# Weights of the first four column groups of each MLP split ahead, kept in DRAM, and loaded as hi and lo parts

## The chip, the cores and the metric

One core of one Trainium2 chip runs the kernel. Its engines are the matmul engine (PE), VectorE (DVE), ScalarE (ACT), GpSimd (POOL) and SyncE (SP), which issues the transfers. The metric is the time of one execution in microseconds on the device, as the median of several runs. All inputs and outputs lie in DRAM, in float32.

## What is computed

A decoder trunk of two layers over 1024 tokens of width 1024. Layer 0 mixes tokens by dilated attention in three head groups, layer 1 by gated linear attention (GLA); behind each mixer stands an MLP of width 4096 with a squared ReLU:

```python
def sq_relu_mlp(h, w_up, w_down):
    a = jax.nn.relu(h @ w_up)
    return (a * a) @ w_down

def reference(x, ...):
    for i in range(DEPTH):
        h = rmsnorm(x, norm_mix_w[i])
        if i % N_MIXERS == 0:
            x = x + dilated_attention(h, attn_w_in[j], attn_w_out[j])
        else:
            x = x + gla_mixer(h, gla_w_in[j], ...)
        h = rmsnorm(x, norm_mlp_w[i])
        x = x + sq_relu_mlp(h, mlp_w_up[i], mlp_w_down[i])
    return rmsnorm(x, final_norm_w)
```

The change concerns the first product of both MLPs, `h @ w_up`.

## The kernel before

**Arithmetic.** A float32 factor is cut in two: ACT rounds it to the short format that PE multiplies (`hi`), and DVE subtracts that from the factor (`lo`). A product is then three matmuls: hi with hi, hi with lo, lo with hi. The large products are moreover done in Strassen's way, as seven products P1 to P7 of quarter matrices in place of eight, so sums and differences of the factors' quarters have to be made first and sums of the products afterwards, on DVE.

**First product of an MLP** (class `Up`). The 4096 columns are done in 16 groups of 256. A group takes seven products of twelve matmuls, each 128x512, in the order P1, P2, P6, P5, P7, P4, P3 (numbered 0 to 6 in `product(p, s)`), into the banks X, Y, X, V, X, Z, V. Bank X is so used three times; between the uses ACT copies it out into a tile `e` (`copy`, line 634), and a product that wants X again waits for that copy. The sums go into `c11` (line 666), `rb` (lines 654 and 668) and `c12` (line 671); `squared` puts each through ReLU and a square on ACT (lines 638 and 639), and `sums` (lines 693 to 698) makes four more sums for the second product. `store` (line 686) writes all of it to DRAM, in `acts`.

**Weights of a group.** `load(p)` fetches the two raw tiles (line 546, 512 KB each), and `stage(p, s)`, in seven steps, makes the hi and lo parts: steps 0 and 1 cut the first column half (`wah`, `wal`), step 2 makes two differences (lines 594 and 595), step 3 cuts them (`wbh`, `wbl`), step 4 makes two more (lines 603 and 604), step 5 cuts those (`wgh`, `wgl`), and step 6 cuts one quarter (`wd`, which holds hi and lo). A cut is a rounding on ACT (line 566) and a subtraction on DVE (line 567).

**Order.** The program is written in the order in which it is to run: each engine executes its own instructions in the order of the code, and waits where one isn't ready. SP issues all transfers, in order too, with at most eight in flight. The stages are: value projections of the attention (class `Values`, 42 steps of 24 matmuls, `prep` of a step two steps ahead), attention heads, output projection (`out_proj`), first MLP (`Halves.finish`, then `Up.run`, then `Down`), then GLA and the same once more for the second MLP, with the final norm at the end of its `Down`. `Down` is the second product of an MLP, 56 steps of 24 matmuls; each step's two factors are loaded five steps ahead (`fetch`, `load`) and cut two steps ahead (`prep`, lines 219 and 222).

The rows of an MLP's input become ready only at the end of `out_proj`, in halves, so the sums of the activations (`s1`, `s2`, `s3`, `a22`, `s4`, lines 378 and 382) are made while the first products run. `Halves.finish` therefore interleaves the products of groups 0 to 3 by hand with these sums and with the staging of the groups' weights; the first groups' loads and first steps stand in `after(tb)`, in `out_proj`. `first_weights` and `first_stage` load and cut the first half of groups 2 and 3 separately. From group 3's P6 on, `Up.run` is a regular loop, with the staging of group p + 1 beside the products of group p.

**Tiles.** The pool `k4` (25 slots of 4 KB per partition) is a ring: raw tiles, weight parts, operand parts of `Down`, and more, each of which waits until the tile that had its slot is done with. `h8` has 12 slots of 8 KB, `t2` 8 of 2 KB; PSUM has 8 banks.

Of the kernel before, what the change touches and what calls it, by code (L numbers as in the profile page):

```python
# [9 lines left out]
F32 = mybir.dt.float32  # L10
F32R = mybir.dt.float32r
# [30 lines left out]
def hybrid_trunk(ctx, tc, x, norm_mix, norm_mlp, norm_fin, a_in, a_out, g_in, g_up, g_b, g_nw,  # L42
# [295 lines left out]
    class Halves:  # L338
# [85 lines left out]
        def after(self, tb):  # L424
            up = self.up
            if tb == 7:
                self.sum1(0)
            if tb % 2:
                self.norm(tb // 2)
            if tb == 1:  # L430
                up.load(0)
            elif tb == 2:
                up.load(1)
            elif tb == 3:
                up.stage(0, 0)
                up.stage(0, 1)
            elif tb == 4:
                up.stage(1, 0)
                up.stage(1, 1)
                up.first_weights(2)  # L440
                up.first_weights(3)
            elif tb == 5:
                up.stage(0, 2)

        def finish(self):
            up, a = self.up, self.a
            P1, P2, P6, P5, P7, P4, P3 = range(7)

            def split(name, src, lo):
                for c in range(2):  # L450
                    self.split(name, src, c, self.one, lo)

            up.product(0, P1)
            self.sum2(0)
            up.done(0, P1)
# [5 lines left out]
            up.first_stage(3)  # L461
            up.product(1, P2)
            up.product(2, P1)
# [20 lines left out]
            up.stage(0, 4)  # L484
            up.product(0, P5)
            split("s3", a[1, 0], self.two)
            up.done(0, P6)
            up.stage(0, 5)
            up.stage(0, 6)
            up.load(2)  # L490
# [5 lines left out]
            up.stage(1, 4)  # L496
            up.product(1, P5)
            up.stage(1, 5)
            up.product(0, P7)
            up.done(0, P7)  # L500
            up.product(0, P4)
            up.stage(1, 6)
            up.stage(2, 2)
            up.stage(2, 3)
            self.sum4()
            up.load(3)
# [4 lines left out]
            up.squared(0, P4)  # L511
            up.product(1, P4)
            up.add(1, P4)
            up.product(2, P6)
            up.stage(2, 4)
# [9 lines left out]
            up.sums(0)  # L525

    NP = FF // 256
    ORDER = ("a12", "a11", "s1", "s2", "s4", "s3", "a22")
# [2 lines left out]
    class Up:  # L531
# [3 lines left out]

        def __init__(self, i):
            self.w = m_up[i]
            self.count = NP
            self.h = {}
            self.raw, self.raw1, self.part, self.t, self.st = {}, {}, {}, {}, {}  # L540

        def load(self, p):
            if p < NP:
# [4 lines left out]
        def first_weights(self, p):  # L548

            if p % 2:  # L550
                r = [t2([P, 4, 128], F32, "raw1") for _ in range(2)]
            else:
                r = r6([P, 2, 4, 128], "raw1")
                r = [r[:, k] for k in range(2)]
            for k in range(2):
                sp.dma_start(r[k], cols(self.w, 256 * p, 128, 4 * k, 4))
            self.raw1[p] = r

        def first_stage(self, p):
            w = self.part.setdefault(p, {})  # L560
            w["a"] = self.two(F32R, "wah"), self.two(F32R, "wal")
            for k, r in enumerate(self.raw1.pop(p)):
                self.cut(*(t[:, k] for t in w["a"]), r)

        def cut(self, hi, lo, src):
            act.activation(hi, src, AF.Copy)  # L566
# [177 lines left out]
    xmid = drp.tile([S, D], F32, name="xmid")  # L744
    acts = [drp.tile([7, 2, P, 512], F32, name=f"acts{m}") for m in range(8)]
    vscr = drp.tile([S, NG, AW], F32, name="vscr")

    class Values:

# [237 lines left out]
    class Heads(Up):  # L987
# [3 lines left out]

        def __init__(self, h):
            self.h = h
            self.raw, self.raw1, self.part, self.t, self.st = {}, {}, {}, {}, {}
# [289 lines left out]
    for n in range(6, 8):  # L1284
# [7 lines left out]
        else:  # L1292
            for c in range(2):
                hs.cut("a22", c)
    vals.load(12)
    for n in range(8, vals.STEPS):
# [145 lines left out]
        st.finish()  # L1442


    class Down:

        def __init__(self, i, next_norm, spill):
            self.w = m_down[i].rearrange("(m j k p) c -> m k p j c", j=2, k=2, p=P)
            self.next_norm, self.spill = next_norm, spill
            self.sin, self.raw, self.cut = {}, {}, {}  # L1450
            self.br, self.tc, self.xs = [], [], [None] * 4
            self.acc = {}
            self.fin = {}
# [88 lines left out]
        def run(self):  # L1542
            ADDS = (None, ("B", 0, 0), ("A", 0, 0), ("B", 1, 1), ("A", 0, 1), ("B", 0, 1), ("A", 1, 0))
            for n in range(54):
                q, m = divmod(n, 8)
                if q and m < 4:
                    s, half, c = ADDS[q]
                    self.add(s, half, m, c)
                    if q == 6:
                        self.add(s, half, m, 1)  # L1550
                self.prep(n + 2)
                self.fetch(n + 5)
                self.load(n + 5)
# [377 lines left out]
```

## Time and profile before

| | us |
|---|---|
| median of 3 runs | 2676.93 |
| lowest and highest | 2676.9, 2678.23 |
| span of the profiled execution | 2672.2 |
| PE busy in it | 2625.7 |
| DVE, ACT, POOL busy | 1787.9, 1238.1, 92.2 |

The span runs from the first to the last instruction that the profile shows; 4.7 us of the median lie outside it. In lists of instructions each row gives the start and duration in us, the engine, the line, the operation and the tiles (output, arrow, inputs), and in brackets how long the engine stood idle before and for whom. Line numbers are those of the kernel before, unless the change is spoken of.

### The profile page before, as it was taken

The numbers are of one execution on the slowest core, as the hardware profiler recorded it, in microseconds if no ns is written. First come the engines' busy times: TensorE is split into PE (matmuls) and PEld (weight loads), VectorE is DVE, ScalarE is ACT, GpSimd is POOL, SyncE is SP. The second block draws the span as 40 slices with busy tenths as digits, with TensorE's granted clock in tenths as the row PEclk, the third lists the DMA queues.
The fourth block names the chain that finished last, engine by engine and source line by source line (L and its number), as shares of the span: only waits on it lengthen the run. The fifth ranks groups of instructions, "written<-read, shape, count | busy, mean of one in ns | idle before, by whom it ended". The sixth has DMA issues, their size and how long they took to land.

```text
span 2672.2 us, 33218 instructions
## 1 busy us (share of the span) xinstructions
PE 2625.7 (98%) x12248; PEld 2175.2 (81%) x12248; DVE 1787.9 (67%) x2944; ACT 1238.1 (46%) x2300; POOL 92.2 (3%) x72
## 2 busy tenths in 40 slices
PE   8999999999999999999999999999999999999998
PEld 6888888888888787888888887778888788888887
DVE  7645878888888677666565672562657766656567
ACT  6323455555555355555533343442425555553343
POOL 0000000000000000000000011321200000000000
PEclk9999999999999999999999999999999999999999
DMA  5443455565557534444856453011223444496543
GB/s 185 165 133 115 116 146 149 145 163 140 152 144 200 187 115 150 158 146 154 308 215 189 137 179 99 24 40 64 91 83 123 153 159 149 139 329 215 185 150 125
DMA packets 311411, 402.16 MB, mean 150 GB/s; under 512 B 18864, under 2 KB 183216, under 8 KB 311248
## 3 DMA queue, kind: packets, MB, share of 16 engines
q1 hardware_dynamic: 311248, 400.04, 47.6%
q8 instruction: 96, 1.57, 0.2%
q14 instruction: 67, 0.55, 0.1%
HBM read 267.13 MB, written 107.68 MB: 140 GB/s over the span
## 4 chain that ended last, share of the span: by engine, by line
PE 80%; DVE 11%; ACT 4%; issue 2%; DMA 2%; SPq 0%; DVEq 0%; ACTq 0%
PE pB L1518 13%; PE pX L629 12%; PE pA L1518 10%; PE pV L629 8%; PE pd L213 5%; PE pd L215 5%; PE pd L214 5%; PE pY L629 4%; PE pB L827 4%; PE pZ L629 4%; PE pA L827 3%; PE pO L960 1%; PE pS L919 1%; DVE c L1013 1%; DMA rows<-og 1%
## 5 line engine op out<-in xcount | busy, mean ns | idle before, releaser
L1518 PE MATMUL pB<-dh 128*128 128x512 f32 x512 | 199.4, 389 | 0.0
L1518 PE MATMUL pB<-dh,dl 128*128 128x512 f32 x512 | 199.2, 389 | 0.0
L1518 PE MATMUL pB<-dl,dh 128*128 128x512 f32 x512 | 199.2, 389 | 0.0
L222 DVE TENSOR_TENSOR dl<-sin,dh 128x1024 fp32r<-128x1024 f32 x112 | 136.6, 1219 | 43.0 <-ACT dh L219 42.5
L219 ACT ACTIVATE dh<-sin 128x1024 fp32r<-128x1024 f32 x112 | 117.8, 1052 | 89.7 <-PE pB L1518 33.5
L935 ACT ACTIVATE pt<-pt,orow 128x128 f32<-128x128 f32 (+1 forms) x192 | 85.0, 444 | 150.2 <-DVE orow L933 148.9
L219 ACT ACTIVATE dh<-kept 128x1024 fp32r<-128x1024 f32 x64 | 67.9, 1061 | 183.3 <-DVE kept L1483 138.0
L629 PE MATMUL pV<-s4h,wd 128*128 128x512 f32 x448 | 150.8, 398 | 0.4 <-ACT e L1050 0.4
L1518 PE MATMUL pA<-dh 128*128 128x512 f32 x384 | 149.4, 389 | 0.0
L1518 PE MATMUL pA<-dl,dh 128*128 128x512 f32 x384 | 149.4, 389 | 0.0
L1518 PE MATMUL pA<-dh,dl 128*128 128x512 f32 x384 | 149.4, 389 | 0.0
L567 DVE TENSOR_TENSOR wbl<-t,wbh 128x1024 fp32r<-128x1024 f32 x56 | 68.6, 1225 | 76.0 <-ACT wbh L566 76.0
L1518 PEld LDWEIGHTS pB<-dl,dh 128*128 128x128 f32 x512 | 96.1, 188 | 20.1
L1518 PEld LDWEIGHTS pB<-dh 128*128 128x128 f32 x512 | 96.1, 188 | 19.9
L1518 PEld LDWEIGHTS pB<-dh,dl 128*128 128x128 f32 x512 | 96.1, 188 | 19.8
L567 DVE TENSOR_TENSOR wal<-raw,wah 128x512 fp32r<-128x512 f32 x112 | 76.2, 686 | 47.8 <-ACT wah L566 47.8
L629 PE MATMUL pX<-s3h,wgh 128*128 128x512 f32 x224 | 93.2, 416 | 11.6 <-ACT e L634 11.6
L638 ACT ACTIVATE c<-c 128x512 f32<-128x512 f32 x64 | 40.4, 632 | 137.6 <-DVE c L666 83.1
L213 PE MATMUL pd<-whi,hTh 128*128 128x512 f32 x256 | 100.5, 393 | 0.0
L148 POOL TENSOR_TENSOR wlo<-raw,whi 128x1024 fp32r<-128x1024 f32 x16 | 40.0, 2500 | 1745.1 <-DMA raw<-in_gla_w_in_dram 1587.7
L215 PE MATMUL pd<-whi,hTl 128*128 128x512 f32 x256 | 99.7, 389 | 0.0
L214 PE MATMUL pd<-wlo,hTh 128*128 128x512 f32 x256 | 99.6, 389 | 0.0
(307 smaller groups left out, 7423.8 us busy)
## 6 DMA issues: line engine op xcount, KB each, us to landing
sin<-acts SPq DMA_DIRECT2D x112, 512.0 KB, 3.9
raw<-in_mlp_w_up_dram SPq DMA_DIRECT2D x64, 512.0 KB, 5.9
acts<-s SPq DMA_DIRECT2D x64, 512.0 KB, 3.4
raw<-in_mlp_w_down_dram SPq DMA_DIRECT2D x64, 512.0 KB, 4.6
raw<-in_attn_w_in_dram SPq DMA_DIRECT2D x96, 256.0 KB, 4.5
cw<-c SPq DMA_DIRECT2D x192, 128.0 KB, 2.3
acts<-c SPq DMA_DIRECT2D x64, 256.0 KB, 2.2
kept<-in_mlp_w_down_dram SPq DMA_DIRECT2D x32, 512.0 KB, 5.3
```

Source lines behind the costliest of these rows:

```text
L148: eng.tensor_tensor(lo, src, hi.bitcast(F32), op=OP.subtract)
L213: pe.matmul(ps, sh, mh, start=start, stop=False)
L214: pe.matmul(ps, sh, ml, start=False, stop=False)
L215: pe.matmul(ps, sl, mh, start=False, stop=stop)
L219: act.activation(hi, src, AF.Copy)
L222: dve.tensor_tensor(lo, src, hi.bitcast(F32), op=OP.subtract)
L567: self.remain(lambda: dve.tensor_tensor(lo, src, hi.bitcast(F32), op=OP.subtract))
L629: pe.matmul(st[b], u[:, k, :], v, start=first and k + n == 0, stop=k == 3 and n == 2, skip_group_check=True)
L638: act.activation(r, r, AF.Relu)
L827: pe.matmul(self.acc[s][t], a[:, c], b[:, k, :], start=fresh and m + k + v == 0, stop=m == 1 and k == 1 and v == 2, skip_group_check=True)
L935: act.activation(pt[:, i, :128 * n], pt[:, i, :128 * n], AF.Exp, scale=-1.0, bias=m, accum_out=self.row[:, r, HD:HD + 1])
L1518: pe.matmul(self.acc[s][t], a[:, k, c], b[:, k, :], start=fresh and m + k + v == 0, stop=m == 7 and k == 1 and v == 2, skip_group_check=True)
```

## The change

For groups 0 to 3 of both MLPs the staging is taken out of `out_proj`, `finish` and `run`. A new class `Ahead` does it in seven steps per group, 28 per MLP (line numbers 535 to 556 of the changed kernel): it loads the two raw tiles, makes the differences in place in them, cuts the same seven parts, and writes them to DRAM, seven tiles of 512 KB per group (`wpre`). A cut's subtraction on DVE and the stores behind it are put off to the next step. MLP 0's 28 steps stand in `Values`, one in each of its steps from 9 on, with the raw tiles in one `h8` slot; to free that slot the load of the rotary table `tab` moves from step 12 to step 38. MLP 1's stand in the `Down` of MLP 0, one in each of its steps 10 to 37, raw tiles in `k4`. `fetch(p, ...)` later loads the parts back: the `a` parts in `after(tb)`, the `b`, `g` and `d` parts in `finish`. `first_weights` and `first_stage` go. The load of group 4 moves from `run` into `finish`.

```diff
         def after(self, tb):
             if tb == 1:
-                up.load(0)
+                up.fetch(0, "a")
             elif tb == 2:
-                up.load(1)
-            elif tb == 3:
-                up.stage(0, 0)
-                up.stage(0, 1)
+                up.fetch(1, "a")
...
         def finish(self):
             up.product(0, P1)
             self.sum2(0)
             up.done(0, P1)
-            up.first_stage(2)
             up.product(0, P2)
-            up.stage(0, 3)
+            up.fetch(0, "b")
...
             up.squared(0, P2)
-            up.stage(1, 2)
-            up.stage(1, 3)
+            up.fetch(0, "g", "d")
...
             up.add(0, P4)
+            up.fetch(2, "g", "d")
             up.product(1, P7)
...
+            up.load(4)
             up.product(2, P5)
-            up.stage(2, 5)
-            up.stage(2, 6)
             up.product(0, P3)
+            up.fetch(3, "g", "d")
             up.product(1, P3)
...
+    class Ahead:
+            def load():
+                r["x"] = self.raw_tiles()
+                for k in range(2):
+                    sp.dma_start(r["x"][k], cols(self.w, 256 * p, 256, 4 * k, 4))
...
+            def cut(hi, lo, src, *stored):
+                act.activation(hi, src, AF.Copy)
+                def rest():
+                    dve.tensor_tensor(lo, src, hi.bitcast(F32), op=OP.subtract)
+                    if stored:
+                        put(*stored)
+                self.behind.append(rest)
...
+            def one():
+                pair("ah", "al")
+                cut(o["ah"][:, 0], o["al"][:, 0], block(0, 0))
+                cut(o["ah"][:, 1], o["al"][:, 1], block(1, 0), "ah", "al")
...
+            def three():
+                less(block(0, 0), block(0, 1), block(0, 0))
+                less(block(0, 1), block(1, 1), block(0, 1))
+                pair("bh", "bl")
+                cut(o["bh"][:, 1], o["bl"][:, 1], block(0, 0))
...
+            self.todo.extend((load, one, two, three, four, five, six))
+
+        def step(self):
+            late = list(self.behind)
+            self.behind.clear()
+            for fn in late:
+                fn()
+            if self.todo:
+                self.todo.popleft()()
...
+        def fetch(self, p, *names):
+            w = self.part.setdefault(p, {})
+            for n in names:
+                got = []
+                for part in ("d",) if n == "d" else (n + "h", n + "l"):
+                    t = self.two(F32R, "w" + part)
+                    sp.dma_start(t.bitcast(F32), self.ahead[p][PARTS.index(part)]
+                                 .rearrange("p (a b c) -> p a b c", a=2, b=4))
...
         def run(self, tail):
             self.product(2, 4)
-            self.stage(3, 2)
             self.product(2, 5)
             self.done(2, 4)
             self.done(1, 6)
-            self.stage(3, 3)
-            self.load(4)
             self.product(2, 6)
             self.done(2, 5)
-            self.stage(3, 4)
-            self.stage(3, 5)
             self.sums(1)
-            self.stage(3, 6)
...
     for n in range(8, vals.STEPS):
-        if n == 12:
+        if n >= 9:
+            ahead.step()
+        if n == vals.STEPS - 4:
             ctab = h8([P, 2, S], F32, "tab")
...
     class Down:
                 self.hook(n)
+                if self.ahead is not None and n >= 10:
+                    self.ahead.step()
                 self.product(n)
```

PE has the same instructions in the same order in both kernels. DVE's rows in MLP 0, from the sum c12 of group 1 (the first row) to that of group 2 (the last), read before, with group 3's staging (lines 567, 603 and 604) among them:

```order
L671 TENSOR_TENSOR c_9254<-pV,e_9031 128x512
L567 TENSOR_TENSOR wbl<-t,wbh 128x1024
L668 TENSOR_TENSOR rb<-pZ,e_9250 128x512
L603 TENSOR_TENSOR t<-raw 128x512
L604 TENSOR_TENSOR t<-raw,t 128x512
L567 TENSOR_TENSOR wgl<-t,wgh 128x1024
L693 TENSOR_TENSOR s_9289<-rb 128x512
L694 TENSOR_TENSOR s_9289<-s_9289,c_8925 128x512
L697 TENSOR_TENSOR s_9293<-c_8925,rb 128x512
L698 TENSOR_TENSOR s_9293<-c_9254,s_9289 128x512
L567 TENSOR_TENSOR wd<-raw,wd 128x512
L671 TENSOR_TENSOR c_9312<-pV,e_9162 128x512
```

In the changed kernel the same stretch of DVE, again from c12 of group 1 to c12 of group 2 (now line 733), reads:

```order
L733 TENSOR_TENSOR c_9409<-pV,e_9196 128x512
L730 TENSOR_TENSOR rb<-pZ,e_9405 128x512
L755 TENSOR_TENSOR s_9430<-rb 128x512
L756 TENSOR_TENSOR s_9430<-s_9430,c_9099 128x512
L759 TENSOR_TENSOR s_9434<-c_9099,rb 128x512
L760 TENSOR_TENSOR s_9434<-c_9409,s_9430 128x512
L733 TENSOR_TENSOR c_9450<-pV,e_9317 128x512
```

Five rows of staging are gone, and what is left are the sums of the products. SP's rows in `finish` of MLP 0 are, before, from the stores of c11 of groups 0 to 3 (line 686) to the first stores of group 0's other results:

```order
L686 DMA acts_82<-c_8923 128x512
L686 DMA acts_82<-c_8925 128x512
L686 DMA acts_83<-c_8964 128x512
L546 DMA raw<-in_mlp_w_up_dram 128x4x256 x2
L686 DMA acts_83<-c_9023 128x512
L546 DMA raw<-in_mlp_w_up_dram 128x4x256 x2
L686 DMA acts_82<-rb 128x512
L686 DMA acts_82<-c_9208 128x512
```

In the changed kernel (line 748 is the store, line 622 the loading back; `wp_1` is group 1), SP has from the stores of c11 of groups 1 and 2 on:

```order
L748 DMA acts_82<-c_9099 128x512
L748 DMA acts_83<-c_9137 128x512
L622 DMA wgh<-wp_1_gh 128x1024
L622 DMA wgl<-wp_1_gl 128x1024
L622 DMA wd<-wp_1_d 128x1024
L748 DMA acts_83<-c_9188 128x512
L622 DMA wbh<-wp_2_bh 128x1024
L622 DMA wbl<-wp_2_bl 128x1024
L622 DMA wgh<-wp_2_gh 128x1024
L622 DMA wgl<-wp_2_gl 128x1024
L622 DMA wd<-wp_2_d 128x1024
```

Group 2's parts moved in behind the last store of c11; behind them come group 3's, group 4's raw tiles and then the stores of group 0's other results. In `Down` of MLP 0, from the first step with a store on, SP of the changed kernel has (line 1527 loads a step's sin, line 1544 its weights):

```order
L543 DMA wp_0_ah<-ah 128x1024
L543 DMA wp_0_al<-al 128x1024
L1527 DMA sin<-acts_84 128x2x512
L1544 DMA kept<-in_mlp_w_down_dram 128x2x512
L543 DMA wp_0_d<-d 128x1024
L1527 DMA sin<-acts_85 128x2x512
L1544 DMA kept<-in_mlp_w_down_dram 128x2x512
L1527 DMA sin<-acts_86 128x2x512
L1544 DMA kept<-in_mlp_w_down_dram 128x2x512
L543 DMA wp_0_bh<-bh 128x1024
L543 DMA wp_0_bl<-bl 128x1024
```

The rows of line 543 are new there; each waits for its part's subtraction on DVE, and the loads of the steps behind it wait with it.

More of the change, by code (lines that the diff above doesn't have):

```diff
@@ L430, in after @@
             if tb == 1:
-                up.load(0)
+                up.fetch(0, "a")
             elif tb == 2:
-                up.load(1)
-            elif tb == 3:
-                up.stage(0, 0)
-                up.stage(0, 1)
+                up.fetch(1, "a")
             elif tb == 4:
[L438 to L443, printed above, removed]
+                up.fetch(2, "a")
+            elif tb == 6:
+                up.fetch(3, "a")
         def finish(self):
@@ L455, in finish @@
             up.done(0, P1)
-            up.first_stage(2)
             up.product(0, P2)
-            up.stage(0, 3)
+            up.fetch(0, "b")
             up.product(1, P1)
             self.turn(3)
-            up.first_stage(3)
             up.product(1, P2)
+            up.fetch(1, "b")
             up.product(2, P1)
@@ L487, in finish @@
             up.done(0, P6)
-            up.stage(0, 5)
-            up.stage(0, 6)
-            up.load(2)
+            up.fetch(1, "g", "d")
             up.product(1, P6)
@@ L495, in finish @@
             up.squared(3, P2)
-            up.stage(1, 4)
+            up.fetch(2, "b")
             up.product(1, P5)
-            up.stage(1, 5)
             up.product(0, P7)
@@ L511, in finish @@
             up.squared(0, P4)
+            up.fetch(3, "b")
             up.product(1, P4)
@@ L537, in __init__ @@
             self.w = m_up[i]
+            self.ahead = wpre[i]
             self.count = NP
             self.h = {}
-            self.raw, self.raw1, self.part, self.t, self.st = {}, {}, {}, {}, {}
+            self.raw, self.part, self.t, self.st = {}, {}, {}, {}
         def load(self, p):
@@ L546, in load @@
                     sp.dma_start(self.raw[p][k], cols(self.w, 256 * p, 256, 4 * k, 4))
[L548 to L559, printed above, removed]
-            w = self.part.setdefault(p, {})
-            w["a"] = self.two(F32R, "wah"), self.two(F32R, "wal")
-            for k, r in enumerate(self.raw1.pop(p)):
-                self.cut(*(t[:, k] for t in w["a"]), r)
+        def fetch(self, p, *names):
+            w = self.part.setdefault(p, {})
+            for n in names:
+                got = []
[3 more added lines that the diff above has]
+                                 .rearrange("p (a b c) -> p a b c", a=2, b=4))
+                    got.append(t)
+                w[n] = got[0] if n == "d" else tuple(got)
         def cut(self, hi, lo, src):
@@ L746, in hybrid_trunk @@
     vscr = drp.tile([S, NG, AW], F32, name="vscr")
+    wpre = [[[drp.tile([P, 1024], F32, name=f"wp{i}_{p}_{n}") for n in PARTS] for p in range(AHEAD)] for i in range(2)]
     class Values:
@@ L993, in __init__ @@
             self.h = h
-            self.raw, self.raw1, self.part, self.t, self.st = {}, {}, {}, {}, {}
+            self.raw, self.part, self.t, self.st = {}, {}, {}, {}
             self.count = HEADS * NG
@@ L1295, in hybrid_trunk, with raw_h8 @@
     vals.load(12)
+    def raw_h8():
+        t = h8([P, 2, 4, 256], F32, "praw")
+        return [t[:, k] for k in range(2)]
+    ahead = Ahead(0, raw_h8, wpre[0])
     for n in range(8, vals.STEPS):
-        if n == 12:
+        if n >= 9:
+            ahead.step()
+        if n == vals.STEPS - 4:
             ctab = h8([P, 2, S], F32, "tab")
@@ L1442, in out_proj, with raw_k4 @@
         st.finish()
+    def raw_k4():
+        return [k4([P, 4, 256], F32, "praw") for _ in range(2)]
     class Down:
@@ L1449, in __init__ @@
             self.next_norm, self.spill = next_norm, spill
+            self.ahead = Ahead(i + 1, raw_k4, wpre[i + 1]) if i == 0 else None
             self.sin, self.raw, self.cut = {}, {}, {}
```

38 lines of the change are left out of this document (32 added, 6 removed).

## The prediction

> **What bounds the kernel now.** The page comes first, for the share of each engine; then all waits of the matmul engine (PE); then windows of 50 us, to see in which stage PE is not full.
>
> ```profile
> span 2672.2 us, 33218 instructions
> PE 2625.7 (98%) x12248; PEld 2175.2 (81%) x12248; DVE 1787.9 (67%) x2944; ACT 1238.1 (46%) x2300; POOL 92.2 (3%) x72
> ...
> PE pT L366 <- DVE xn L256: 12.0, 7, 10.6
> PE pX L629 <- ACT e L634: 11.6, 2, 5.8
> PE pX L629 <- DVE wbl L567: 1.1, 2, 0.5
> ...
> 1000.00:1050.00 50.00, 49.47 (x217) 40.13 (x216) 39.76 (x56) 31.06 (x40) 0.00 (x0) 1.00 0.37 123
> 1050.00:1100.00 50.00, 44.23 (x186) 36.32 (x186) 34.91 (x52) 23.84 (x36) 0.00 (x0) 0.93 0.56 189
> 1100.00:1150.00 50.00, 50.00 (x222) 41.42 (x221) 30.87 (x45) 25.56 (x37) 0.00 (x0) 1.00 0.39 131
> 2100.00:2150.00 50.00, 43.67 (x183) 34.73 (x183) 35.03 (x51) 24.75 (x34) 0.00 (x0) 0.93 0.57 194
> ```
>
> PE is busy for 98% of the span, so work taken off DVE or ACT is worth only what PE waits for it. The first wait (12.0 us, 10.6 in one piece) is the start of the program, which the change leaves alone. The next two are what it touches: two waits of 5.8 us, one per MLP, for line 634 (ACT's copy that empties bank pX), and two of 0.5 for a low part of line 567. In a window row, behind the stretch and its length, stand the busy times of PE, weight loads, DVE, ACT and GpSimd, then the granted clock, the DMA share and GB/s. Outside the two stretches PE fills its window at clock 1.00; inside it has 44 of 50 us, at 0.93. So the change can win back one place in each MLP, and elsewhere it can only cost.
>
> The place, from the timelines of PE, ACT and DVE:
>
> ```profile
> 1040.60 0.68 DVE L671 TENSOR_TENSOR c<-pV,e 128x512 f32<-128x512 f32 x1
> 1042.52 1.04 ACT L566 ACTIVATE wbh<-t 128x1024 fp32r<-128x1024 f32 x1
> 1043.59 1.23 DVE L567 TENSOR_TENSOR wbl<-t,wbh 128x1024 fp32r<-128x1024 f32 x1 [2.31 <-ACT wbh L566]
> 1043.61 0.50 PE L629 MATMUL pX<-s2h,wbh 128*128 128x512 f32 x1
> 1047.28 0.39 PE L629 MATMUL pV<-s1h,wbh 128*128 128x512 f32 x1
> 1048.58 1.23 DVE L567 TENSOR_TENSOR wgl<-t,wgh 128x1024 fp32r<-128x1024 f32 x1 [1.97 <-ACT wgh L566]
> 1049.72 0.69 DVE L693 TENSOR_TENSOR s<-rb 128x512 f32<-128x512 f32 x1
> 1052.26 0.69 DVE L567 TENSOR_TENSOR wd<-raw,wd 128x512 fp32r<-128x512 f32 x1
> 1052.86 0.68 DVE L671 TENSOR_TENSOR c<-pV,e 128x512 f32<-128x512 f32 x1
> 1053.58 0.63 ACT L638 ACTIVATE c<-c 128x512 f32<-128x512 f32 x1 [4.51 <-DVE c L671]
> 1055.30 0.58 ACT L634 ACTIVATE e<-pX 128x512 f32<-128x512 f32 x1
> 1055.92 0.80 PE L629 MATMUL pX<-s3h,wgh 128*128 128x512 f32 x1 [5.77 <-ACT e L634]
> ...
> 1055.92 5.19 PE pX L629 x12
> 1061.12 2.72 PE pZ L629 x12
> ```
>
> I write 3P7 for product P7 of group 3. 3P7 needs pX, which the copy e (1055.30) empties of 3P6. That copy has had its data since 3P6 ended at about 1047; it stands on ACT behind the square of group 2's c12 (1053.58), and that square waits 4.51 us for the DVE add at 1052.86. DVE could have done this add as soon as group 2's P3 was in its bank, at 1043.6, where 3P6 begins. It stands behind the staging of group 3's weights: between 1043.59 and 1052.86 each cut on DVE waits for a rounding on ACT, and the roundings stand on ACT behind squares that wait for DVE. The two engines go in turns, both with idle time, and PE pays: 5.77 us of waiting, then twelve matmuls that take 5.19 us, where the twelve after them take 2.72.
>
> **What goes.** Loss of the stretch = first matmul of 3P4 (pZ) less first of 3P6, less three products of 2.72. MLP 0: 1061.12 - 1043.61 - 8.16 = **9.35 us** (0.95 in 3P6, where wbl is late; 5.92 before 3P7; 2.47 in the slow matmuls). MLP 1, from the same two matmuls:
>
> ```profile
> 2106.72 0.50 PE L629 MATMUL pX<-s2h,wbh 128*128 128x512 f32 x1
> 2119.03 0.80 PE L629 MATMUL pX<-s3h,wgh 128*128 128x512 f32 x1 [5.80 <-ACT e L634]
> 2123.34 0.40 PE L629 MATMUL pZ<-a22h,wgh 128*128 128x512 f32 x1
> ```
>
> 2123.34 - 2106.72 - 8.16 = **8.46 us**. Together 17.8. PE's instructions and their order are the same in both kernels, so this is all that can be won.
>
> Is all of it won? The staging of groups 0 to 3 leaves DVE: per group two cuts of 1.23 and seven operations of 0.69 us, 7.3 us, 29 us per MLP, most of it in the interleaved part ahead of this place. What is left in front of the copy, from 1040.6 on, at DVE's pitch of 0.6 us (1052.26 to 1052.86): group 2's P4 sum, ready when PE ends that product, at 1043.61 - 2.72 = 1040.9; its two passes on ACT of 1.04 each (as wbh, equally wide), to about 1044; four sums on DVE, not waited for; the c12 add at 1043.7 to 1044.3; its two passes on ACT, to 1045.7; then the copy, which now waits for 3P6 itself: 1046.33 to 1046.95 at unbroken pace. 3P7 is due at 1043.61 + 2 x 2.72 = 1049.05. That leaves 2.1 us, so I book both losses as gone. With the gap goes the slow clock: the twelve matmuls before it had no gap and the window row shows 1.00.
>
> By the Trainium skill (TensorE: Matmul & The Clock Gate, on the clock's activity window), an idle window of about 3.4 us halves the clock until PE has been busy as long again. The trace agrees: after 5.77 us twelve matmuls took 5.19 instead of 2.72. By that rule a gap shortened to 2 us would cost only itself; by a rule in proportion it would cost 2.9. With the gap gone both give the sum below; they differ for a late fetch, the second rival.
>
> **What is added, by place.** Per group there are 11 DVE and 7 ACT operations on 512 columns, 2 loads and 7 stores of 512 KB; so per MLP 44 x 0.69 = 30 us of DVE, 28 x 0.6 = 17 us of ACT, 4.2 MB read and 14.7 MB written, over 28 steps of 5.44 us = 152 us. Later come 28 loads, 14.7 MB.
>
> ```profile
> 72.00:232.00 160.00, 160.00 (x707) 132.50 (x706) 81.56 (x86) 49.99 (x67) 0.00 (x0) 1.00 0.41 136
> 1295.00:1349.00 54.00, 54.00 (x240) 44.72 (x239) 36.96 (x36) 29.05 (x30) 0.00 (x0) 1.00 0.96 351
> 1349.00:1509.00 160.00, 160.00 (x707) 132.48 (x707) 93.02 (x86) 57.23 (x56) 0.00 (x0) 1.00 0.55 181
> ...
> 250.00:300.00 50.00, 50.00 (x233) 41.68 (x232) 36.78 (x66) 17.35 (x37) 0.00 (x0) 1.00 0.45 124
> ...
> L827 PE MATMUL pB<-dl,s4h 128*128 128x512 f32 x48 | 18.8, 391 | 0.5 <-DVE dl L812 0.5
> L222 DVE TENSOR_TENSOR dl<-sin,dh 128x1024 fp32r<-128x1024 f32 x112 | 136.6, 1219 | 43.0 <-ACT dh L219 42.5
> ```
>
> *Value projections* (MLP 0's part): DVE 82 + 30 = 112 of 160 us, ACT 50 + 17 = 67, transfers 136 + 18.9 MB / 152 us = 260 GB/s. All three fit beside a PE that is full and that DVE feeds with steps of its own to spare. The one wait of PE there is 0.5 us, for a dl (its group's row above). I book 0; bounds -0.5 (that wait goes, since the table load moves from step 12 to 38) and +2 (it comes once for each group).
>
> *Down product of MLP 0* (MLP 1's part, steps 10 to 37): DVE 93 + 30 = 123 of 160, ACT 57 + 17 = 74, transfers 181 + 124 = 305 GB/s. The stage's first 54 us carry 351 GB/s at share 0.96 with PE full, so the rate has been sustained here without harm. What gets thinner is the lead of the split tiles: with raw tiles and pairs of the new work in the same ring of 25 slots, a step's splits wait for the slots of the product three steps before it where now they wait for one four or five before. That leaves two steps, 10.9 us, for splits of two roundings (1.04 each) and two cuts (1219 ns in the row above), some 5 us with a sum. I book +1, bounds 0 and +20 (four groups of 5 us).
>
> *Loading back.* SP issues in order, so a fetch stands behind the stores of c11 ahead of it, at about the times these have now.
>
> ```profile
> 942.15 0.38 SPq L354 DMA_DIRECT2D xmid<-xs  x1
> 979.21 0.39 PE L629 MATMUL pX<-a11h,wah 128*128 128x512 f32 x1
> 998.77 7.52 SPq L686 DMA_DIRECT2D acts<-c  x3
> 1013.64 0.39 PE L629 MATMUL pX<-s3h,wgh 128*128 128x512 f32 x1
> 1014.19 0.34 SPq L686 DMA_DIRECT2D acts<-c  x1
> ...
> sin<-acts SPq DMA_DIRECT2D x112, 512.0 KB, 3.9
> raw<-in_mlp_w_up_dram SPq DMA_DIRECT2D x64, 512.0 KB, 5.9
> ...
> sin<-acts SPq DMA_DIRECT2D x12, 512.0 KB, 8.8
> ```
>
> The a parts are asked for from 942 on and needed at 979. Group 0's g and d follow the store at 998.8, land at about 1006, and 0P7 needs them at 1013.64. Tightest is group 2's b: behind the last c11 store, at 1014.6, landing at 1020.5 (5.9, the price of an equal raw load); 2P6 comes four products after 0P7, at 1013.64 + 10.88 = 1024.5. That leaves 4 us, and still 1 at the 8.8 us that the most crowded loads took (the last row, of window 1295 to 1349). Group 3's parts are needed 19 us or more later. Booked at 0; bounds 0 and +6 for both MLPs.
>
> **Sum.** -17.8 + 0 + 1 + 0 = -16.8. The profiled execution's span of 2672.2 and 4.7 around it are 2676.9, the median itself: 2676.9 - 16.8 = **2660 us**.
>
> **Rivals.**
> 1. *Half is given back in Down.* Four times the rounding of a group's first half stands on ACT before its raw tile has landed, and the steps' own roundings behind it. It is asked for one step earlier, late in that step's work, and lands after 6 to 9 us, so ACT may stand for 4 to 8 us where the slack is 5 or 6. For: the thin ring. Against: sin, of the same size, lands in 3.9 over the whole kernel. At 2 to 4 us per group: 2659 + 8 to 2659 + 16, **2667 to 2675**.
> 2. *A late fetch takes the place of the stall*: group 2's b or g lands 3 us late in each MLP, 6 us in all, **2666**; were the slow clock to come with it, 2 us more each time (2.47 and less above), 2670. Against: the 4 us above.
> 3. *The stall stays*: the copy e is late for a reason that is not staging, say a square that waits for a store's buffer, or group 4's staging, which stays and whose raw load now comes behind fetches. Then the two gaps shrink by a few us at best: **2672 to 2677**. Against: all DVE work between 1043.59 and 1052.86 but the four sums is staging.
> 4. *Slower: Down becomes bound by its transfers.* The 28 steps then need 181 x 0.1523 = 27.6 + 18.9 = 46.5 MB in 152 us. Below 305 GB/s PE waits; at 273 GB/s the whole gain is gone (46.5 / 0.273 = 170 us); below 266 the kernel is over 0.2% slower. Window 250 to 300, with small packets, has 124 GB/s at share 0.45, that is 275 when full; stores mixed among loads could go as low. At 262 GB/s: 177.5 us, +25, **2685**. Against: 181 / 0.55 = 329 GB/s in this very stage.
>
> **Chances.** Forecast 0.62 (its own range 2656 to 2664), given back 0.16, late fetch 0.04, stall stays 0.08, slower 0.10. A measurement of this kernel can tell about 0.2%, 5.4 us, from no change, so faster means below 2671.5: 0.62 + 0.04 + 0.11 of the case given back = 0.77; same 0.05 + 0.08 = 0.13; slower 0.10. The range, 2656 to 2672, takes in the forecast, the late fetch and most of what is given back, some 0.78.
>
> **What would show it.** Right: no wait of PE on pX for e in either MLP, PE at 50.0 of 50 and clock 1.00 in 1050 to 1100, DVE's add for group 2's c12 within a us of 1043.6, and Down's 56 steps still at 5.44 us. Wrong: a PE wait for dl or dh in Down, or steps longer than 5.44 us at DMA share near 1 (rivals 1 and 4); a PE wait whose releaser is a DMA into wbh or wgh (rival 2); the old wait for e (rival 3). What would undo the forecast outright is PE waiting in the value projections, where I book nothing.

## The result, and the profile after

| | before | changed |
|---|---|---|
| median, us (4 runs each) | 2677.14 | 2657.98 |
| lowest and highest | 2676.9, 2678.23 | 2657.38, 2659.44 |
| span of the profiled execution | 2672.2 | 2655.9 |

The ratio is 0.9925, with a 95% interval of 0.9911 to 0.9939: faster by 0.75%, 19.2 us of the medians and 16.3 us of the two spans. The forecast was 2660.

From the page of the changed kernel come the span and the engines' shares; the next rows are the longest waits of PE over the whole span (in total, times, longest), and the last two are the windows of the two places, which the earlier start of MLP 1 has moved.

```profile
span 2655.9 us, 33487 instructions
PE 2622.3 (99%) x12248; PEld 2174.9 (82%) x12248; DVE 1789.6 (67%) x2960; ACT 1238.6 (47%) x2316; POOL 91.3 (3%) x72
...
PE pT L366 <- DVE xn L256: 11.7, 7, 10.3
PE pd L214 <- DVE wlo L148: 2.3, 3, 1.8
PE pk L1906 <- DVE kdT L1901: 2.0, 1, 2.0
...
1050.00:1100.00 50.00, 50.00 (x221) 41.20 (x220) 30.98 (x45) 26.13 (x38) 0.00 (x0) 1.00 0.49 163
2080.00:2130.00 50.00, 50.00 (x221) 41.23 (x220) 32.18 (x48) 24.90 (x34) 0.00 (x0) 1.00 0.64 225
```

DVE and ACT have as much to do as before; what is gone are the waits on pX, and PE fills both places at clock 1.00. The timelines of DVE, ACT and PE in MLP 0 show how (line 733 is the sum c12, first of group 1, then of group 2; line 696 copies pX):

```profile
1039.40 0.68 DVE L733 TENSOR_TENSOR c<-pV,e 128x512 f32<-128x512 f32 x1
1043.42 0.69 DVE L760 TENSOR_TENSOR s<-c,s 128x512 f32<-128x512 f32 x1
1044.02 0.68 DVE L733 TENSOR_TENSOR c<-pV,e 128x512 f32<-128x512 f32 x1
1044.74 0.63 ACT L700 ACTIVATE c<-c 128x512 f32<-128x512 f32 x1 [0.98 <-DVE c L733]
1046.46 0.58 ACT L696 ACTIVATE e<-pX 128x512 f32<-128x512 f32 x1
...
1043.40 0.39 PE L691 MATMUL pX<-s2h,wbh 128*128 128x512 f32 x1
1051.56 0.39 PE L691 MATMUL pZ<-a22h,wgh 128*128 128x512 f32 x1
...
2099.03 0.39 PE L691 MATMUL pX<-s2h,wbh 128*128 128x512 f32 x1
2107.19 0.39 PE L691 MATMUL pZ<-a22h,wgh 128*128 128x512 f32 x1
```

Group 2's c12 comes 4.6 us behind group 1's, where it came 12.3 behind, and the copy of pX is over at 1047.04, before 3P7 wants the bank. From 3P6 to 3P4 PE takes 1051.56 - 1043.40 = 8.16 us, in MLP 1 2107.19 - 2099.03 = 8.16: three products without a gap.

The stages that took over the work, in the windows that the prediction used:

```profile
72.00:232.00 160.00, 160.00 (x708) 132.56 (x707) 107.85 (x130) 64.98 (x95) 0.00 (x0) 1.00 0.75 258
1349.00:1509.00 160.00, 160.00 (x708) 132.51 (x707) 125.03 (x134) 72.05 (x83) 0.00 (x0) 1.00 0.84 292
```

PE is full in both, with DVE up by 26 and 32 us and the transfers at 258 and 292 GB/s. The work was not saved; it went to where it costs nothing.

### The profile page after: what moved, and what is told of

Same layout as the page of the kernel before. It is cut to its first block, busy times and chain, and to the rows that moved or that the text cites. A ratio compares the mean times of both kernels' runs of the same rounds, so it can differ in the third digit from the quotient of the medians.

```text
span 2655.9 us, 33487 instructions
## 1 busy us (share of the span) xinstructions
PE 2622.3 (99%) x12248; PEld 2174.9 (82%) x12248; DVE 1789.6 (67%) x2960; ACT 1238.6 (47%) x2316; POOL 91.3 (3%) x72
## 4 chain that ended last, share of the span: by engine, by line
PE 87%; DVE 7%; ACT 2%; issue 2%; DMA 2%; SPq 0%; DVEq 0%; ACTq 0%
PE pX L691 15%; PE pB L1586 13%; PE pA L1586 10%; PE pV L691 10%; PE pd L213 5%; PE pd L215 5%; PE pd L214 5%; PE pY L691 5%; PE pZ L691 5%; PE pB L884 4%; PE pA L884 3%; PE pS L976 2%; PE pO L1017 1%; DVE c L1070 1%; DMA rows<-og 1%
## 5 line engine op out<-in xcount | busy, mean ns | idle before, releaser
L696 ACT ACTIVATE e<-pX 128x512 f32<-128x512 f32 x96 | 56.5, 589 | 104.5 <-PE pX L691 104.5
L629 DVE TENSOR_TENSOR wbl<-t,wbh 128x1024 fp32r<-128x1024 f32 x48 | 58.8, 1225 | 66.9 <-ACT wbh L628 66.9
L691 PEld LDWEIGHTS pV<-s4h,wd 128*128 128x128 f32 x448 | 84.2, 188 | 18.7 <-ACT e L1107 1.3
```

Of the source, the lines that this page charges most:

```text
L629: self.remain(lambda: dve.tensor_tensor(lo, src, hi.bitcast(F32), op=OP.subtract))
L691: pe.matmul(st[b], u[:, k, :], v, start=first and k + n == 0, stop=k == 3 and n == 2, skip_group_check=True)
L696: act.activation(e, self.st[p]["X"], AF.Copy)
```

## Experiments

Both kernels' PE work is the same, so where a run loses or gains can be read from the start of each matmul, counted from the first, in two traces. That matters, since the attention heads alone shift by up to 3 us from one trace to the next. Each run was timed on one chip beside the kernel before. The question of the first three: is it group 3's staging that blocks (theory A), or the amount of work (theory B)?

**Only group 3 ahead.** The kernels here hold both ways of getting a group's weights, and a list says which groups go ahead:

```diff
-    AHEAD = 4
+    AHEAD = ((3,), (3,))
```

> Only group 3 of each MLP is split ahead and loaded back; groups 0 to 2 are staged in place as before. Theory A (the two waits on pX come from group 3's staging alone, which stands on DVE and ACT between the sums c12 of groups 1 and 2): nearly the whole gain, 15 to 18 us of the span, PE waiting under 1 us per MLP. Theory B (what counts is how much DVE work leaves the stretch, whichever group's): a quarter of the gain, 4 to 6 us.

Measured: 2657.7 us against 2676.66, ratio 0.9928 (0.9913 to 0.9943); PE has no wait in either MLP. This is the whole gain, with 415.8 MB moved in place of 458.8 (402.2 before): a quarter of the added traffic. Theory A holds against B.

**Groups 0 to 2 ahead, group 3 in place.**

```diff
-    AHEAD = 4
+    AHEAD = ((0, 1, 2), (0, 1, 2))
```

> Groups 0 to 2 are split ahead, group 3 is staged in place as before. Theory A: the turns of DVE and ACT over group 3's three cuts remain; by hand the copy of pX comes at about 1053.5 to 1054.1 where it came at 1055.3 to 1055.9, so the wait is still 4 to 5 us per MLP with the slow clock behind it, and 2 to 5 us are gained in all, most of it in 3P6. Theory B: three quarters of the gain, 12 to 14 us.

Measured: 2673.23 us against 2676.66, ratio 0.999 (0.998 to 0.9999), some 3 us, which is A's size; in the traces 2.2 us of it lie in the two MLPs. The waits on pX did not shrink to 4 or 5 us as expected, though. The rows (PE's waits, DVE, ACT; line 788 is c12 there, line 751 the copy, line 684 a cut's low part):

```profile
PE pX L746 <- ACT e L751: 11.4, 2, 5.8
...
1034.99 0.69 DVE L788 TENSOR_TENSOR c<-pV,e 128x512 f32<-128x512 f32 x1 [6.20 <-PE pV L746]
1044.67 1.23 DVE L684 TENSOR_TENSOR wbl<-t,wbh 128x1024 fp32r<-128x1024 f32 x1 [2.31 <-ACT wbh L683]
1049.66 1.23 DVE L684 TENSOR_TENSOR wgl<-t,wgh 128x1024 fp32r<-128x1024 f32 x1 [1.97 <-ACT wgh L683]
1054.65 0.63 ACT L755 ACTIVATE c<-c 128x512 f32<-128x512 f32 x1 [4.51 <-DVE c L788]
1056.37 0.58 ACT L751 ACTIVATE e<-pX 128x512 f32<-128x512 f32 x1
```

Three quarters of the staging are gone, and DVE has nothing to do for 6.2 us before it meets group 0's c12. Then it runs through the same turns with ACT (2.31, 1.97, 4.51 us of waiting, the very numbers of before) and the copy is as late as ever. Work taken out ahead of a place where the engine waits for PE anyway only makes that wait longer.

**The same, with group 3's staging written into that idle time.** Nothing is taken away against the run before:

```diff
             up.product(1, P3)
+            for k in range(2, 7):
+                up.stage(3, k)
             up.add(0, P3)
...
         def run(self, tail):
             self.product(2, 4)
-            self.stage(3, 2)
             self.product(2, 5)
```

(and so for steps 3 to 6 in `run`.)

> Groups 0 to 2 split ahead as in the run before; group 3 is staged in place, but its steps 2 to 6 are written ahead of the sum c12 of group 0, where the run before has DVE idle for 6.2 us (1028.8 to 1035.0). No work is taken away against that run. Theory A (what costs is that group 3's staging stands between the sums of groups 1 and 2): both waits on pX go, 15 to 18 us gained against the kernel before, as with all four groups ahead. Theory B (it is the amount of DVE and ACT work of the whole stretch): no gain over that run, 0 to 4 us against the kernel before.

Measured: 2663.28 us against 2677.45, ratio 0.9948 (0.9934 to 0.9963), 14.2 us, a little under A's 15 to 18. The waits on pX are down to 0.5 us in all; 1.7 and 1.5 us are left at the next place, where PE waits for rb of group 3. So, with groups 0 to 2 ahead, it is the place of this work that counts, not its amount in the whole stretch.

**Can order alone do it, with nothing ahead?** The kernel before, with `run` written in another order:

```diff
             self.done(2, 4)
-            self.done(1, 6)
             self.stage(3, 3)
+            self.done(1, 6)
             self.load(4)
             self.product(2, 6)
-            self.done(2, 5)
             self.stage(3, 4)
             self.stage(3, 5)
-            self.sums(1)
-            self.stage(3, 6)
+            self.done(2, 5)
+            self.product(3, 2)
+            self.add(2, 6)
+            self.done(3, 2)
+            self.squared(2, 6)
+            self.stage(3, 6)
+            self.sums(1)
...
```

> The kernel before, nothing split ahead; only the written order of the run of groups 2 and 3 is changed: group 3's roundings stand on ACT ahead of the squares of groups 1 and 2, the add of c12 of group 2 and the copy of pX ahead of that square, and the four sums of group 1 behind. Theory A in its strict form (it is the place in the queues, not the amount of work): the copy of pX ends by about 1048, so 14 to 18 us are gained with no byte moved. Theory B (DVE and ACT are too full there): under 6 us.

Measured: 2681.93 us, ratio 1.0015 (1.0005 to 1.0024): no gain, rather a loss. The wait on pX is gone as computed, and another has come (PE's waits):

```profile
PE pV L629 <- DVE rb L654: 14.5, 2, 7.2
...
PE pX L629 <- ACT e L634: 1.5, 2, 0.8
```

3P7 started 8.0 us earlier than before, and 3P3, two products on, waited 7.2 us for DVE's rb, which stood behind the sums and group 4's staging. A second order put rb ahead of these and delayed the sums of groups 1 and 2:

```diff
+            self.product(3, 3)
+            self.stage(4, 0)
+            self.stage(4, 1)
+            self.product(3, 4)
+            self.done(3, 4)
+            self.sums(1)
+            self.stage(4, 2)
...
+            self.product(3, 5)
+            self.done(3, 5)
+            self.sums(2)
+            self.load(5)
...
```

> Nothing split ahead; the written order of the first reordered kernel, and behind it also rb of group 3 and group 4's first cuts ahead of the sums of groups 1 and 2. There PE waited 7.2 us per MLP for rb of group 3, which DVE did at 1060.1 behind 10 us of sums and of group 4's staging. If the order alone decides, that wait goes as well and 14 to 18 us are gained against the kernel before. If DVE and ACT are behind by an amount of work that no order hides, the wait moves on to the next product that wants a tile (group 4's parts or its sums) and less than 6 us are gained.

Measured: 2680.53 us, ratio 1.001 (1.0001 to 1.002). The wait moved on once more:

```profile
PE pX L629 <- ACT e L634: 16.5, 4, 7.7
```

two small ones of group 3 and two of 7.3 and 7.7 us before group 4's P6, which wants pX from group 4's P1 (the expectation that follows names it P7). Theory A in its strict form, that the place of group 3's staging alone decides, has fallen with these two. In its stead I put theory C: from 1035 to 1070 DVE and ACT, which go in turns, have about one group's staging too much; an order chooses which product pays.

**Another group's staging away, in this order.** If C is right, group 4 serves as well as group 3. The first trial took the first order with only group 4 ahead:

> The first reordered kernel (groups 0 to 3 staged in place, group 3's staging put ahead of the sums), and only group 4 of each MLP split ahead and loaded back. Theory C (from about 1035 to 1070 DVE and ACT, which go in turns, have some 8 us too much to do; an order only moves the wait from 3P7 to 3P3 or to group 4's P7, and one group's staging less in that stretch, whichever group's, is enough): the wait of 7.2 us for rb of group 3 goes as well and 13 to 17 us are gained against the kernel before. Theory A in its strict form (group 3's staging alone is the trouble): PE still waits 5 us or more per MLP, as in the two reordered kernels, and the time is that of the kernel before or slower.

Measured: 2671.2 us against 2676.87, ratio 0.9983 (0.9974 to 0.9993). The wait for rb of group 3 is gone, as C had it, but the gain is 5.7 us and not 13 to 17: by a slip the copy of pX for group 3 was written twice, and 3P7 waited 2.9 us for the second in each MLP. Without the slip, and in the second order:

> The second reordered kernel (rb of group 3 ahead of the sums), with only group 4 of each MLP split ahead and loaded back, and with one copy of pX for group 3 (the run before had made it twice by a slip, and 3P7 waited for the second). Theory C (some 8 us of DVE and ACT work too much from 1035 to 1070; an order moves the wait, one group's staging less, whichever group's, removes it): 13 to 17 us gained against the kernel before, PE waits in the MLPs under 1 us each. Theory A in its strict form (only group 3's staging matters): the wait stays at group 4's P7 or comes at another place, 5 us or more per MLP, and nothing is gained.

Measured: 2678.98 us against 2676.66, ratio 1.0011 (1.0002 to 1.0021). That looked like the end of C, until ACT's and DVE's rows were read (line 683 rounds, wah here belongs to group 5):

```profile
PE pX L746 <- ACT e L751: 16.4, 4, 7.5
...
1059.16 0.68 DVE L788 TENSOR_TENSOR c<-pV,e 128x512 f32<-128x512 f32 x1
1069.41 0.63 ACT L683 ACTIVATE wah<-raw 128x512 fp32r<-128x512 f32 x1 [8.23 <-DMA raw<-in_mlp_w_up_dram]
1069.94 0.58 ACT L751 ACTIVATE e<-pX 128x512 f32<-128x512 f32 x1
1070.07 0.69 DVE L684 TENSOR_TENSOR wal<-raw,wah 128x512 fp32r<-128x512 f32 x1 [10.22 <-ACT wah L683]
```

Here neither engine had too much to do: both stood idle for 8 to 10 us. ACT had come to group 5's first rounding, whose raw tile was asked for only at 1060.0, and the copy of pX stood behind it. The wait has the length and the place of that in the second reordered kernel, and another cause. One edit more:

```diff
             self.squared(2, 6)
             self.stage(3, 6)
             self.fetch(4, "b")
+            self.load(5)
...
             self.sums(2)
-            self.load(5)
```

> The run before, with one change: the load of group 5's raw tiles stands ahead of the sums of groups 1 and 2. There DVE was idle for 10.2 us and ACT for 8.2 while ACT stood for that raw tile, with the copy of pX for group 4 behind it; the transfer had been asked for at 1060.0, behind the store of sums. If that late load alone made the wait of 7.5 us per MLP, it goes: 13 to 17 us gained against the kernel before with only group 4 split ahead, which is theory C (one group's staging less, whichever, does it in a fitting order). If the wait stays at 5 us or more with the raw tile there in time, theory C falls, and only group 3's staging counts.

Measured: 2659.78 us against 2676.63, ratio 0.9941 (0.9924 to 0.9958), 16.9 us; PE's waits on pX are 1.5 us in all:

```profile
PE pX L746 <- ACT e L751: 1.5, 2, 0.8
```

C fits all runs: one group's staging less between the end of group 2 and the start of group 5 is enough, group 3's in the written order, or group 4's in an order that suits it. A late load was not what stopped the second order with nothing ahead; that order with the early load was not run. Its rows (ACT, DVE, and the window with both engines' busy times):

```profile
1067.94 0.63 ACT L566 ACTIVATE wah<-raw 128x512 fp32r<-128x512 f32 x1 [0.23 <-DMA raw<-in_mlp_w_up_dram]
1065.70 0.68 DVE L671 TENSOR_TENSOR c<-pV,e 128x512 f32<-128x512 f32 x1
1035.00:1070.00 35.00, 26.98 (x116) 21.59 (x115) 24.75 (x37) 18.09 (x25) 0.00 (x0) 0.93 0.59 203
```

ACT stood only 0.23 us for the raw tile. "Too much" is not a lack of engine time either: DVE was busy for 24.75 of 35 us and ACT for 18.09. It is the old picture one group later: group 3's c12, whose product 3P3 ended at 1056.2, was added at 1065.70, behind the turns over group 4's staging. Two orders with all groups staged in place did not help; whether another one would stays open.

**How near was the second product to its limit?** Two splitting steps to a step of `Down`:

```diff
                 if self.ahead is not None and n >= 10:
                     self.ahead.step()
+                    self.ahead.step()
```

> The changed kernel, but MLP 1's 28 steps of splitting run two to a step of the second product of MLP 0 (its steps 10 to 23), so that the transfers asked for there are 181 + 248 = 429 GB/s and DVE has about 0.58 x 160 + 60 of the same stretch. If the margin of that product is in the rate of transfers (rival 4): at some 390 GB/s the 14 steps stretch from 76 to 84 us, 8 us slower than the changed kernel. If it is in the ring of slots (rival 1): 4 waits of 2 to 5 us, 8 to 20 us. If there is more margin than I reckoned: within 2 us of it, 2658.

Measured: 2676.79 us, ratio to the kernel before 1.0005 (0.9995 to 1.0015): the gain is gone, 18.8 us against the changed kernel. Against the trace of that one, 14.9 us are lost between 1394 and 1430. ACT's waits in 1290 to 1450, the window where PE is short, and a row of ACT:

```profile
ACT ah L547 <- DMA praw<-in_mlp_w_up_dram: 28.9, 8, 7.5
...
1392.00:1442.00 50.00, 41.07 (x157) 31.34 (x155) 37.74 (x44) 23.07 (x29) 0.00 (x0) 0.90 0.88 307
...
1394.52 0.63 ACT L547 ACTIVATE ah<-praw 128x512 fp32r<-128x512 f32 x1 [7.53 <-DMA praw<-in_mlp_w_up_dram]
```

SP issued that raw tile's load at 1389.3, 5 us before the rounding. Is it this, or the rate? One run keeps the rate of one step and starts with step 0 of `Down`, on top of the 351 GB/s there:

```diff
-                if self.ahead is not None and n >= 10:
+                if self.ahead is not None:
```

> The changed kernel, but MLP 1's 28 steps of splitting start with the first step of the second product of MLP 0 and not with its step 10, so that ten of them fall into the 54 us that carry 351 GB/s at DMA share 0.96 already. If the transfers set the margin, as the run with two steps at a time showed (PE waited once the share stood near 0.9 and ACT stood 7.5 us for a raw tile): 475 GB/s are asked of about 390, 10 to 14 us slower than the changed kernel. If the loads five steps ahead absorb it: within 2 us of it.

Measured: 2662.57 us against 2677.45, ratio 0.9942 (0.9924 to 0.9959). My 10 to 14 us did not come: in all of `Down` PE waited 0.3 us. The run is 4.6 us slower than the changed kernel all the same, which is over the 2 us of the other expectation; of the 5.5 us between the two traces 1.0 lies in `Down`, 1.2 ahead of it and 3.2 in GLA, at two gaps where the clock fell (last section). Windows of that run:

```profile
1320.00:1340.00 20.00, 20.00 (x90) 16.56 (x89) 12.83 (x14) 8.94 (x10) 0.00 (x0) 1.00 1.05 401
1360.00:1380.00 20.00, 20.00 (x90) 16.57 (x89) 14.01 (x15) 6.77 (x8) 0.00 (x0) 1.00 1.05 396
```

Transfers at 401 GB/s, with landings of 10.3 us for a sin (median, 1300 to 1345), and PE full. The other run keeps two steps to a step and asks for each group's raw tiles a group earlier:

```diff
             def one():
+                if i and self.loads:
+                    self.loads.popleft()()
                 pair("ah", "al")
...
```

> The kernel with two splitting steps to a step of the second product, but each group's raw tiles are asked for a whole group earlier. If what cost 16 us there was ACT standing up to 7.5 us for a raw tile that had been asked for only half a step before (rival 1): at most 5 us are left against the changed kernel. If it was the rate of the transfers or the ring of slots (rival 4, or the thin ring): 10 us or more stay, since as many bytes go and two more slots are held.

Measured: 2664.44 us against 2676.87, ratio 0.9956 (0.9939 to 0.9973); 6.5 us above the changed kernel, between the two expectations. By the traces 4.5 us of the 14.9 are left in `Down`; the rest lies in the heads and in GLA. ACT waited for a raw tile twice where it had waited eight times:

```profile
ACT ah L548 <- DMA praw<-in_mlp_w_up_dram: 8.2, 2, 7.4
```

So most of what twice the pace cost in `Down`, 10.4 of 14.9 us, was ACT standing, in order, for a tile that was asked for late. The rate alone was not the limit, since PE stayed full at 401 GB/s; what the other 4.5 us are stays open.

No version beat the changed kernel. The one with only group 3 ahead equals it with a quarter of the added bytes.

## Why the prediction was right, and where it was off

- **What goes**: 17.81 us, computed as the two stretches from 3P6 to 3P4 less three products each. Measured: both stretches are 8.16 us long, so all of it went. The copy of pX, computed for 1046.33 to 1046.95, ran from 1046.46 to 1047.04; group 2's c12, computed for 1043.7, came at 1044.02. The turns of DVE and ACT over group 3's staging were the cause, as the runs with group 3 alone and with groups 0 to 2 show.
- **The slow clock** went with the gap, in both MLPs (1.00 in the windows). That a gap of 2 us costs only itself, as the prediction drew from the Trainium skill (TensorE: Matmul & The Clock Gate, on the clock's activity window), did not hold in GLA: one of 2.05 us cost 1.6 us more (last section).
- **Value projections**, booked at 0: right. DVE 107.9 of 160 us (112 computed), ACT 65.0 (67), 258 GB/s (260). The wait of 0.5 us that the lower bound had going is there as before.
- **Down**, booked at +1: it cost 0, with DVE at 125 (123), ACT at 72 (74) and 292 GB/s over the window. The first rival's mechanism exists, and twice the pace brings it out; at the pace of the change ACT's waits for raw tiles (3.7 us at the longest) stay inside the lead.

```profile
ACT ah L547 <- DMA praw<-in_mlp_w_up_dram: 11.9, 6, 3.7
```

- **The fourth rival**, a limit by the rate of transfers, did not come: `Down` got its 292 GB/s, and 401 where more was asked. Its bound of 275 GB/s, a quiet window's rate divided by its share, was no limit; the fullest window, 351 / 0.96 = 366 GB/s, would have been the better guide, though 401 passed that too.
- **Late fetch**: group 2's b was asked for at 1013.17 (computed 1014.6). The slowest landing of a wbh in this stage took 8.1 us, so it was there by 1021.3, and 2P6 began at 1024.4: at least 3 us to spare, 4 computed.

```profile
1013.17 0.38 SPq L622 DMA_DIRECT2D wbh<-wp_bh  x1
...
DMA to landing us min/median/max: 3.9/6.4/8.1
L691 PE MATMUL pX<-s2h,wbh x4: 389/389/390, 1024.4 to 1026.4; 128*128 128x512 f32 x4
```

- **The base** was wrong by some 3 us. All four runs of the changed kernel lie 1.8 us above their span, where I had put 4.7 around that of before: its span of 2672.2 and its median belong to different executions. The 25 executions of the kernel before that were timed beside the run with group 3 alone lie 1.8 above their spans too. So the profiled one took 2674.0 us, a short one among those 25 (2672.56 to 2679.49), and this is why the medians differ by 19.2 and the spans by 16.3. The spread of 7 us goes with the clock on record: the seven executions with a mean granted clock of 0.996 or 0.997 took 2672.6 to 2674.5 us, the eighteen with 0.994 or 0.995 took 2675.8 to 2679.5.
- **The sum by spans** closes: 17.8 won in the MLPs, 1.6 lost in GLA, 16.3 measured, with 0.2 of scatter ahead of the MLPs. The loss is the last section's; no term of the prediction had it. That 2660 came so near is in part luck: the base and the 1 us for `Down` made it 3.9 too high, and the 1.6 that it left out took part of that back.

## What to carry to other kernels

Where two in-order engines hand halves of one operation to each other, look for the place where both show idle time and PE waits at its end, and ask which work stands between the result that PE needs and the moment its inputs were there; that work alone is worth moving, and a quarter of it moved here gave all the gain. Two other orders within this stretch only moved the wait to a later product; it went when one group's work left the stretch or was written into an idle time ahead of it. A wait of the same length at the same line is not yet the same wait: the row of the engine that is waited for tells its cause. Here work could be put beside a full PE at up to 401 GB/s of transfers, and cost time where a tile was asked for shortly before the instruction that stood in the queue for it.

## What the runs showed of the hardware

The clock fell after a gap of 2 us in one execution and not in another. In GLA PE waits once for kdT, in both kernels alike; rows of the kernel before, then of the changed one (the matmul behind the gap, then windows):

```profile
1714.05 0.66 PE L1836 MATMUL pk<-ident,kdT 128*128 128x128 f32 x4 [2.08 <-DVE kdT L1831]
1709.17:1712.58 3.41, 2.81 (x13) 1.99 (x11) 3.31 (x4) 0.47 (x1) 3.41 (x2) 1.00 0.00 0
1712.58:1715.99 3.41, 1.94 (x11) 1.68 (x12) 2.58 (x3) 0.00 (x0) 2.21 (x2) 1.00 0.00 0
1715.99:1719.40 3.41, 3.41 (x13) 2.01 (x12) 1.55 (x7) 3.25 (x9) 1.80 (x3) 1.00 0.00 0
...
1704.80 1.03 PE L1906 MATMUL pk<-ident,kdT 128*128 128x128 f32 x4 [2.05 <-DVE kdT L1901]
1701.53:1704.94 3.41, 1.36 (x7) 0.82 (x6) 3.11 (x3) 0.00 (x0) 3.41 (x3) 1.00 0.00 0
1704.94:1708.35 3.41, 3.41 (x11) 2.83 (x11) 1.65 (x4) 1.52 (x5) 1.79 (x3) 0.50 0.00 0
1708.35:1711.76 3.41, 3.41 (x13) 1.97 (x12) 1.16 (x4) 1.73 (x5) 0.61 (x1) 1.00 0.00 0
```

After 2.08 us the clock stayed at 1.00; after 2.05 it stood at 0.50 for 3.41 us, with the matmuls 0.43 us apart from 1705.48 to 1708.19. It cost 1.6 us, which no step of the change accounts for. The difference is where the gap falls. In all 13 traces of this case the granted clock changes only at points of a grid of 3.41 us, and the windows above lie on each trace's own grid. The gap of 2.08 us was split between two windows, with PE busy for 2.81 and 1.94 us; that of 2.05 lay in one, with 1.36. Counted over all 13 traces, from 30 to 2640 us: of the 37 grid windows at full clock with PE busy for less than 1.6 of the 3.41 us, 34 were followed by a window at half clock, and of some 9,800 fuller ones a single one (1.67 us). So what counted here was PE busy for less than about half of a window, not the length of the gap.

The Trainium skill (TensorE: Matmul & The Clock Gate, on the activity window) has a free-running window of about 3.4 us, and the traces agree with it. The rule of the Trainium skill (same page, on how the gate bites in real kernels) against idle gaps of more than about 3.4 us is too lenient for this case, where 2.05 us was enough. In the traces of other runs the same happened at two more gaps of GLA, near 1780 and 1990, at about 1.6 us each; part of what the runs differ by comes from there.

Transfers of one core reached 401 GB/s over 20 us at a DMA share of 1.05, with stores and loads mixed, and a load of 512 KB (a sin) then took 10.3 us to land where the kernel before has 3.9 over the whole run.
